# Seven quarter products for eight column pairs of the first up projection, with weight sums added in place by DMAs

## The chip, the cores and the metric

The kernel runs on one core of a Trainium2 chip. Its time is the device time of one execution in microseconds (us). TensorE (PE) multiplies, VectorE (DVE) and ScalarE (ACT) do elementwise work and read PSUM, GpSimd (POOL) does a few additions and can issue DMAs, and SyncE (SP) issues nearly all DMAs. PSUM holds the sums of the matmuls in banks; SBUF holds everything else.

## The reference

A trunk of two decoder layers works on 528 tokens (16 learned ones before 512) of width 1024, all in float32. Each layer is a mixer (one combined projection, four retention heads and four heads of gated linear attention, an output projection) and a gated MLP, each between two RMS norms. The change is in the MLP of the first layer:

```python
def _conv_ffn(h, ffn_up, ffn_conv_w, ffn_conv_b, ffn_down):
    length = h.shape[1]
    u = h @ ffn_up                                   # (528, 1024) @ (1024, 5632)
    up = jnp.pad(u, ((0, 0), (CONV_W - 1, 0), (0, 0)))
    conv = ffn_conv_b + sum(up[:, i:i + length] * ffn_conv_w[i] for i in range(CONV_W))
    a, g = jnp.split(conv, 2, axis=-1)
    return (jax.nn.gelu(a, approximate=True) * g) @ ffn_down
```

The 5632 columns are 22 blocks of 128 for `a` and 22 for `g`. Block i of `a` meets block i of `g` in the product behind the GELU, so the kernel works through 22 column pairs.

## The kernel before

Activations lie with the feature on the partitions and the 528 tokens along the free axis. Precision of float32 is kept by splitting: each activation and each weight is a sum of two float16 numbers, and a product is three matmuls (high x high, high x low, low x high), added up in one PSUM bank (`product_step`, L410). The normalised input of a projection is `xh`, eight tiles (k = 0 to 7) of high and low parts.

A weight block (`Block`, L80) is 1024 rows by 128 columns, 512 KB. SP loads it into a staging buffer (eight of them in layer 0); ACT writes its scaled high part into a *unit* (L110) and DVE its low part (L111). There are ten units. `plan` (L593) lists all blocks in the order of use, and `block` (L622) hands out one of them and, before that, asks for the next ten (`AHEAD`), so loads and conversions run ahead of the matmuls as far as staging buffers and units are free.

`ffn_up` (L1033) goes through the column pairs. `one(key, i, half)` multiplies one block with one part of the tokens (232 in the first half, 296 in the second): 24 matmuls into one of three PSUM banks, which ACT then copies to SBUF as `u` (L1058). `finish(col)` does the convolution of both columns (`conv`: one pass on ACT, L1042, and two on DVE, L1047), the GELU (L1098), and, one pair later, the product and its split into float16 (L1109, L351, L352). The first five pairs (`ULEAD`) run their first token half before the second, because the second half of the norm before them is still on its way; the other pairs run both halves in turn. `tick()` takes one step of whatever generator of background work is waiting.

The order of instructions on each engine is written out by hand only for the opening of the kernel; after it a planner orders them by program order and its own estimates of durations. At run time every engine, and every queue that issues DMAs, takes its instructions strictly in the planned order.

The last down projection (`last_down`) already uses the scheme that the change brings to the up projection: seven products of quarter matrices in place of eight, with sums of weights (there made by DVE, L144) and sums of activations. `w11` to `t4` and `r1`, `r5`, `u2` are its names.

Of the kernel before, what the change touches and what calls it, by code (L numbers as in the profile page):

```python
# [20 lines left out]
DEPTH = 2  # L21
INW = 3600
DFF = 2816
KF = DFF // P
# [7 lines left out]
WN = max(272, L - SPLIT)  # L32
LEVELS = [1, 2, 4, 8, 16, 32, 64]
SX = 8.0
SW = 128.0
SA = 8.0
IXW = 1.0 / (SX * SW)
# [4 lines left out]
UNITS = 10  # L42
# [3 lines left out]
ULEAD = 5  # L46
# [13 lines left out]
HK = KF // 2  # L60
HT = SEQ // 2
PRODUCTS = (("w11", "t1"), ("t2",), ("w22", "t3"), ("w21",), ("t4",))
KPARTS = ((0, 8), (8, 8), (16, 6))


# [5 lines left out]
def cell(pool, shape, dt, tag, name, bufs=None):  # L71

    n = math.prod(shape[1:])
    size = 2 if dt == F16 else 4
    t = pool.tile([shape[0], -(-n * size // CELL) * CELL // size], dt, tag=tag, name=name, **({"bufs": bufs} if bufs else {}))[:, :n]
    names = "abcdef"[: len(shape) - 1]
    return t if len(names) == 1 else t.rearrange(f"p ({' '.join(names)}) -> p {' '.join(names)}", **dict(zip(names, shape[1:])))


class Block:  # L80


    def __init__(self, kern, layer, src, nk, c0, w):
        self.kern, self.src, self.nk, self.c0, self.w = kern, src, nk, c0, w
        self.unit = self.st = None
        self.ahead = 99
        self.layer = layer

    def load(self):
        if self.w < P:  # L90
            st = self.st = self.kern.rank.rearrange("p (k c) -> p k c", c=self.w)
        else:
            st = self.st = cell(self.kern.stage, [P, KD, self.w], F32, *self.kern.stage_of(self.layer))[:, : self.nk]
        load = self.kern.nc.sync.dma_start(st, self.src[:, self.c0 : self.c0 + self.w].rearrange("(k p) c -> p k c", p=P))
        if self.layer:
            self.kern.tc.keep_in_program_order(load)

    def fetch(self):
        if self.unit is not None:
            return  # L100
        nc = self.kern.nc
        if self.st is None:
            self.load()
        st = self.st
        if self.w < P:
            self.unit = cell(self.kern.wpool, [P, self.nk, P // (2 * self.w), 2, self.w], F16, "unit", "unit", UNITS)
            u = self.unit[:, :, 0].rearrange("p k i c -> p i k c")
        else:
            u = self.unit = cell(self.kern.wpool, [P, 2, KD, self.w], F16, "unit", "unit", UNITS)[:, :, : self.nk]
        nc.scalar.activation(u[:, 0], st, AF.Copy, scale=SW)  # L110
        nc.vector.scalar_tensor_tensor(out=u[:, 1], in0=st, scalar=SW, in1=u[:, 0], op0=ALU.mult, op1=ALU.subtract)  # L111
        if self.w < P:
            for j in range(1, self.unit.shape[2]):
                nc.gpsimd.tensor_copy(out=self.unit[:, :, j], in_=self.unit[:, :, 0])


class Quarter:
# [22 lines left out]
    def fetch(self):  # L140
        if self.unit is not None:
            return
        kern, nc, kk = self.kern, self.kern.nc, self.kk
        add = lambda to, x: kern.tc.keep_in_program_order(nc.vector.tensor_tensor(out=to, in0=to, in1=x, op=ALU.add))  # L144
        if self.what == "w11":
            x = self.acc["w11", kk] = self.load(kern.w11_place(kk))
        elif self.what == "w22":
            x = self.acc["w22", kk] = self.load()
        elif self.what == "w21":
            x = self.load()  # L150
        else:
            x = self.acc.pop(("w22", kk)) if self.what == "t3" else self.acc["w11", kk]
            add(x, self.load())
        self.unit = cell(kern.wpool, [P, 2, 2, 512], F16, "unit", "unit", UNITS)[:, :, : self.nk]
        high = nc.scalar.activation(self.unit[:, 0], x, AF.Copy, scale=SW)
        if self.what in ("w11", "t1"):
            kern.tc.keep_in_program_order(high)
        nc.vector.scalar_tensor_tensor(out=self.unit[:, 1], in0=x, scalar=SW, in1=self.unit[:, 0], op0=ALU.mult, op1=ALU.subtract)


class Kern:
# [105 lines left out]
    def mm(self, shape, name="mm"):  # L267
        return self.pmm.tile(shape, F32, tag="mm", name=name)
# [324 lines left out]
    def plan(self):  # L593
        a = self.a
        self.blocks, self.key = [], {}

        def add(key, *args):
            self.key[key] = len(self.blocks)
            self.blocks.append(Block(self, key[0], *args))

        cols = {"rk": C_RK, "rq": C_RQ, "rv": C_RV, "rg": C_RG, "gk": C_GK, "gq": C_GQ, "gv": C_GV, "gr": C_GR}
        for l in range(DEPTH):
            for nm, h in TILES:
                add((l, nm, h), a["w_in"][l], KD, *((C_GA, 16) if nm == "ga" else (cols[nm] + P * h, P)))
            for i in range(KD):
                add((l, "out", i), a["w_out"][l], KD, P * i, P)
            for i in range(KF):
                add((l, "upa", i), a["ffn_up"][l], KD, P * i, P)
                add((l, "upg", i), a["ffn_up"][l], KD, DFF + P * i, P)
            if l < DEPTH - 1:  # L610
                for i in range(KD):
                    for kk, nk in KPARTS:
                        add((l, "dn", i, kk), a["ffn_down"][l][kk * P : (kk + nk) * P], nk, P * i, P)
            else:
                acc = {}
                for group in PRODUCTS:
                    for kk in range(0, HK, 2):
                        for what in group:
                            self.key[l, "dn", what, kk] = len(self.blocks)
                            self.blocks.append(Quarter(self, a["ffn_down"][l], what, kk, min(2, HK - kk), acc))  # L620
# [390 lines left out]
    def out_proj(self, l):  # L1011
# [18 lines left out]
        self.finish(gens[0])  # L1030
        self.xh, self.later = xh, gens[1]

    def ffn_up(self, l):  # L1033
        nc = self.nc
        base = 0 if l < DEPTH - 1 else 14
# [2 lines left out]
        us = {}  # L1038

        def conv(u, c, col):  # L1040
            ci = lambda i: 88 + (l * 3 + i) * 44 + col
            nc.scalar.activation(c[:, lo:L], u[:, lo:], AF.Identity, scale=self.cvec[:, ci(2) : ci(2) + 1],  # L1042
                                 bias=self.cvec[:, l * 44 + col : l * 44 + col + 1])
            for i in (1, 0):
                d = 2 - i
                to = c[:, max(lo, d) :]
                nc.vector.scalar_tensor_tensor(out=to, in0=u[:, max(lo, d) - d : L - d], scalar=self.cvec[:, ci(i) : ci(i) + 1],  # L1047
                                               in1=to, op0=ALU.mult, op1=ALU.add)
# [13 lines left out]
        keep, parts = {}, {nm: [None] * HK for nm in ("x11", "x12", "x22", "s1", "s2", "s3", "s4")}  # L1062
# [52 lines left out]
        for half in range(2):  # L1115
            for i in range(ULEAD):
                one("upa", i, half)
                one("upg", i, half)
                if half:
                    finish(i)  # L1120
            if half == 0:
                self.finish(self.later)
        for i in range(ULEAD, KF):
            for half in range(2):
                one("upa", i, half)
                one("upg", i, half)
            finish(i)
# [3 lines left out]
    def ffn_down(self, l, av):  # L1131
# [176 lines left out]
```

## Time and profile before

| | us |
|---|---|
| median of 3 runs | 1251.44 |
| lowest and highest run | 1250.09, 2556.68 |
| profiled execution, device time | 1250.15 |
| its span in the trace | 1248.4 |
| PE busy | 1227.0 |
| DVE busy | 806.5 |
| ACT busy | 654.2 |
| POOL busy | 157.1 |

The profiled execution lies within 0.1% of the median; the 1.8 us between its time and its span lie outside the trace. Times within the trace count from the start of the span. A row of a group of instructions names its line, engine, operation, the tiles it writes and reads, its shape and count; behind the first bar stand busy time and the mean duration in ns, behind the second the idle time of the engine just before, and what ended it. A row of a stretch gives its length, then the busy time (and count) of PE, the weight loads of PE, DVE, ACT and POOL, then PE's granted clock, the busy share of the DMA engines and the GB/s they moved. A matmul's duration in the trace contains its way through the array; matmuls overlap, so their pace is read from their number in a stretch. The first up projection runs from about 288 to 530 us.

### The profile page before, as it was taken

What the parts mean: (1) busy time and instruction counts of PE and PEld (TensorE: products, weight loads), DVE (VectorE), ACT (ScalarE), POOL (GpSimd) and SP (SyncE); (2) the same over time, 40 slices, a digit from 0 to 9 for tenths busy, and PEclk for the clock granted to TensorE, in tenths of its full rate; (3) what the DMA queues carried; (4) which work ended last, traced back from release to release, by engine and by line L of the source; (5) the groups of instructions that cost most, each with busy time, mean ns of one, the idle gap of its engine ahead of it and who ended that gap; (6) DMA issues with size and microseconds to landing.
All of it is one profiled execution on the core that took longest, in us unless ns stands there. A gap on an engine that the chain in (4) does not pass through costs nothing.

```text
span 1248.4 us, 26366 instructions
## 1 busy us (share of the span) xinstructions
PE 1227.0 (98%) x11106; PEld 1017.4 (81%) x11106; DVE 806.5 (65%) x1414; ACT 654.2 (52%) x1290; POOL 157.1 (13%) x206
## 2 busy tenths in 40 slices
PE   8999999999999999999999999999999999999997
PEld 8788888889888888888878888888798888886443
DVE  5577744467876666613186878434669768887686
ACT  5675445454865555523255744453638556664442
POOL 1012211153000000000032222011520000000001
PEclk9999999999999999999999999999999999999999
DMA  7932221131533333315052332212315333305461
GB/s 203 264 108 86 68 70 52 51 101 36 153 102 94 94 94 93 93 42 139 14 157 73 98 86 67 71 52 69 102 35 153 102 102 102 119 1 181 149 236 68
DMA packets 206827, 124.18 MB, mean 99 GB/s; under 512 B 6688, under 2 KB 194132, under 8 KB 206708
## 3 DMA queue, kind: packets, MB, share of 16 engines
q1 hardware_dynamic: 206548, 121.97, 33.2%
q8 instruction: 87, 1.43, 0.5%
q0 software_dynamic: 160, 0.52, 0.2%
q14 instruction: 32, 0.26, 0.1%
HBM read 120.38 MB, written 2.10 MB: 98 GB/s over the span
## 4 chain that ended last, share of the span: by engine, by line
PE 92%; DVE 3%; POOL 2%; ACT 1%; issue 1%; DVEq 0%; POOLq 0%; ACTq 0%
PE pu L414 12%; PE pu L415 12%; PE pu L413 12%; PE pl L1173 8%; PE pj L413 8%; PE pj L415 7%; PE pj L414 7%; PE pd L413 3%; PE pd L414 3%; PE pd L415 3%; PE po L413 2%; PE po L415 2%; PE po L414 2%; PE lps L841 1%; DVE unit L111 1%
## 5 line engine op out<-in xcount | busy, mean ns | idle before, releaser
L414 PE MATMUL pu<-every,unit 128*128 128x296 f16 (+2 forms) x1408 | 385.7, 275 | 2.1 <-DVE every L352 2.1
L415 PE MATMUL pu<-every,unit 128*128 128x296 f16 (+2 forms) x1408 | 385.7, 275 | 0.0
L413 PE MATMUL pu<-every,unit 128*128 128x296 f16 (+2 forms) x1408 | 384.1, 275 | 0.7 <-ACT every L351 0.7
L111 DVE SCALAR_TENSOR_TENSOR unit<-st,unit 128x1024 f16<-128x1024 f32 x184 | 227.1, 1234 | 162.0 <-ACT unit L110 156.3
L413 PEld LDWEIGHTS <-unit 128*128 128x128 f16 x2912 | 284.7, 98 | 49.2 <-issue 6.9
L415 PEld LDWEIGHTS <-unit 128*128 128x128 f16 x2912 | 284.6, 98 | 46.4 <-issue 3.1
L414 PEld LDWEIGHTS <-unit 128*128 128x128 f16 x2912 | 284.9, 98 | 41.5 <-issue 0.2
L110 ACT ACTIVATE unit<-st 128x1024 f16<-128x1024 f32 x184 | 191.5, 1041 | 127.9 <-PE pu L415 52.6
L415 PE MATMUL pj<-every,unit 128*128 128x296 f16 (+2 forms) x896 | 246.4, 275 | 0.7 <-DVE unit L111 0.7
L413 PE MATMUL pj<-every,unit 128*128 128x296 f16 (+2 forms) x896 | 246.7, 276 | 0.0
L414 PE MATMUL pj<-every,unit 128*128 128x296 f16 (+2 forms) x896 | 246.6, 275 | 0.0
L1058 ACT ACTIVATE u<-pu 128x296 f32<-128x296 f32 (+2 forms) x176 | 66.3, 379 | 95.9 <-PE pu L415 95.8
L415 PE MATMUL pd<-av,unit 128*128 128x232 f16 (+1 forms) x352 | 96.9, 276 | 0.0
L414 PE MATMUL pd<-av,unit 128*128 128x296 f16 (+1 forms) x352 | 96.8, 276 | 0.0
L413 PE MATMUL pd<-av,unit 128*128 128x232 f16 (+1 forms) x352 | 96.8, 276 | 0.0
L379 DVE TENSOR_TENSOR acc<-acc,sq 128x296 f32<-128x296 f32 (+2 forms) x60 | 33.3, 556 | 78.5 <-ACT sq L377 76.5
L347 POOL TENSOR_TENSOR every<-every 128x1 f32<-128x1 f32 (+5 forms) x33 | 38.9, 1181 | 289.2 <-DVE every L346 192.0
L1173 PE MATMUL pl<-unit,fk 128*128 128x512 f16 x330 | 71.4, 379 | 0.0
L1047 DVE SCALAR_TENSOR_TENSOR cg<-u,every,cg 128x527 f32<-128x527 f32 (+1 forms) x88 | 66.5, 756 | 5.5 <-ACT cg L1042 4.3
L415 PE MATMUL po<-merged,unit 128*128 128x296 f16 (+2 forms) x256 | 69.9, 275 | 0.0
L414 PE MATMUL po<-merged,unit 128*128 128x296 f16 (+2 forms) x256 | 69.9, 275 | 0.0
L413 PE MATMUL po<-merged,unit 128*128 128x296 f16 (+2 forms) x256 | 69.7, 275 | 0.0
(225 smaller groups left out, 1502.4 us busy)
## 6 DMA issues: line engine op xcount, KB each, us to landing
st<-in_ffn_up SPq DMA_DIRECT2D x88, 512.0 KB, 3.7
st<-in_w_in SPq DMA_DIRECT2D x56, 512.0 KB, 4.1
st<-in_ffn_down SPq DMA_DIRECT2D x46, 512.0 KB, 3.7
st<-in_w_out SPq DMA_DIRECT2D x16, 512.0 KB, 4.0
st<-in_ffn_down SPq DMA_DIRECT2D x8, 384.0 KB, 3.1
out<-yo SPq DMA_DIRECT2D x8, 256.0 KB, 2.0
xt<-in_x SPq DMA_DIRECT2D x6, 256.0 KB, 6.3
w<-in_ffn_down SPq DMA_DIRECT2D x3, 512.0 KB
```

The costliest lines, as they stand in the source:

```text
L110: nc.scalar.activation(u[:, 0], st, AF.Copy, scale=SW)
L111: nc.vector.scalar_tensor_tensor(out=u[:, 1], in0=st, scalar=SW, in1=u[:, 0], op0=ALU.mult, op1=ALU.subtract)
L347: nc.gpsimd.tensor_tensor(out=r[:w, :n], in0=t[:w, :n], in1=self.mhalf[:w, :n], op=ALU.pow)
L379: eng.tensor_tensor(out=acc[:, :n], in0=acc[:, :n], in1=sq[:, :n], op=ALU.add)
L413: nc.tensor.matmul(ps[:, :n], w[:, 0, kk, :], x[:, 0, n0:n1], start=first, stop=False)
L414: nc.tensor.matmul(ps[:, :n], w[:, 0, kk, :], x[:, 1, n0:n1], start=False, stop=False)
L415: nc.tensor.matmul(ps[:, :n], w[:, 1, kk, :], x[:, 0, n0:n1], start=False, stop=last)
L841: nc.tensor.matmul(dst, x[hs, i, c0 : c0 + w], q, start=(i, j) == (0, 0), stop=i == 1)
L1047: nc.vector.scalar_tensor_tensor(out=to, in0=u[:, max(lo, d) - d : L - d], scalar=self.cvec[:, ci(i) : ci(i) + 1], in1=to, op0=ALU.mult, o ...
L1058: nc.scalar.activation(u[:, n0:n1], ps[:, : n1 - n0], AF.Copy, scale=IXW)
L1173: mm = lambda x, w, **kw: nc.tensor.matmul(ps, x, w, skip_group_check=more, **kw)
```

## The change

In layer 0 the column pairs 7, 9, 11, ... 21 are computed together, `a` block and `g` block as one product of a 1024 x 256 weight with the 528 tokens. All three dimensions are cut in two: rows in 2 x 512 (four k each), columns into the two blocks, tokens in 2 x 264. The four quarter results come out of seven quarter products of 4 k x 3 matmuls each, instead of eight. In the names of the last down projection, with W_ab the quarter of row half a and column block b:

- step 0: w11 = W00 and w22 = W11, loaded by SP into the two halves of a staging buffer
- step 1: t1 = W00 + W01 and t3 = W11 + W01, by two DMAs that POOL issues and that add W01 from DRAM to what lies in the buffer
- step 2: t2 = t1 + W11, by one more adding DMA, and w21 = W10, loaded by SP over t3
- step 3: t4 = t2 + W10, by one more adding DMA

Each step is converted to float16 (ACT, then DVE) into a unit of its own, half a unit for step 3, before the next step changes the buffer. So a pair has four blocks in the plan's list in place of two. `input_sums` makes the four sums of the activations once, on DVE and ACT, as background work during the second token half of the first five pairs. `paired` does the seven products in two banks that are added to after they were read (`pa`: products 1, 3, 5 and 7, `pb`: 2 and 4) and a third (`pd`: product 6); ACT copies the intermediate values r1, r5, u2 and the last result out, DVE forms the other three results from PSUM and those copies. Layer 1 and the other pairs stay as they are.

```diff
+PAIRED = {0: range(7, KF, 2), 1: ()}
+HK2 = KD // 2
+LT = L // 2
...
+class PairPiece:
...
+    def fetch(self):
+        if self.unit is not None:
+            return
+        kern, nc = self.kern, self.kern.nc
+        load = lambda to, *q: nc.sync.dma_start(to, self.quarter(*q))
+        add = lambda to, *q: nc.gpsimd.dma_start(out=to, in_=self.quarter(*q), accum_op=ALU.add)
+        if self.step == 0:
+            self.st = cell(kern.stage, [P, 2, HK2, P], F32, *kern.stage_of(self.layer))
+        st = self.first.st
+        if self.step == 0:
+            load(st[:, 0], 0, 0)
+            load(st[:, 1], 1, 1)
+        elif self.step == 1:
+            add(st[:, 0], 0, 1)
+            add(st[:, 1], 0, 1)
+        elif self.step == 2:
+            add(st[:, 0], 1, 1)
+            load(st[:, 1], 1, 0)
+        else:
+            add(st[:, 0], 1, 0)
+            st = st[:, :1]
+        u = self.unit = cell(kern.wpool, [P, 2, 2, HK2, P], F16, "unit", "unit", UNITS)[:, :, : st.shape[1]]
+        nc.scalar.activation(u[:, 0], st, AF.Copy, scale=SW)
+        nc.vector.scalar_tensor_tensor(out=u[:, 1], in0=st, scalar=SW, in1=u[:, 0], op0=ALU.mult, op1=ALU.subtract)
...
+    def input_sums(self):
...
+        for k in range(0, KD, 2):
+            nc.vector.tensor_tensor(out=xf[:, k : k + 2], in0=xh[:, k : k + 2, 0], in1=xh[:, k : k + 2, 1], op=ALU.add)
+            yield
...
+            nc.vector.tensor_tensor(out=to, in0=x0, in1=x1, op=op)
+            t = parts[:, (2, 0, 1, 3)[i]]
+            nc.scalar.activation(t[:, 0], to, AF.Copy)
+            nc.vector.tensor_tensor(out=t[:, 1], in0=to, in1=t[:, 0], op=ALU.subtract)
+            yield
+
+    def paired(self, units, scale, out):
...
+        def product(ps, step, i, x, more=False):
+            u = units(step)[:, :, i]
+            for k in range(HK2):
+                mm = lambda p, q, **kw: nc.tensor.matmul(ps, u[:, p, k, :], x[k][:, q], skip_group_check=more, **kw)
+                mm(0, 0, start=k == 0 and not more, stop=False)
+                mm(0, 1, start=False, stop=False)
+                mm(1, 0, start=False, stop=k == HK2 - 1)
+            self.tick()
...
+        pa, pb = bank(), bank()
+        product(pa, 0, 0, half(0, 0))
+        r1 = copied(pa)
+        product(pb, 1, 0, self.xsum[1])
+        r5 = copied(pb)
+        product(pa, 2, 0, self.xsum[2], True)
+        u2 = copied(pa)
+        product(pb, 0, 1, self.xsum[4], True)
+        sum_to(1, 0, pb, u2, 1.0, ALU.subtract)
+        product(pa, 1, 1, self.xsum[3], True)
+        sum_to(1, 1, pa, r5, -1.0, ALU.add)
+        pd = bank()
+        product(pd, 2, 1, half(HK2, 0))
+        sum_to(0, 0, pd, r1, 1.0, ALU.add)
+        product(pa, 3, 0, half(HK2, 1), True)
+        nc.scalar.activation(out[0][:, LT:], pa, AF.Copy, scale=scale)
...
         for i in range(ULEAD, KF):
+            if i in PAIRED[l]:
+                for key in ("upa", "upg"):
+                    us[key, i] = cell(self.gen, [P, L], F32, "u", "u", 2 * ULEAD)
+                self.paired(lambda q: self.block(l, "pair", i, q), IXW, (us["upa", i], us["upg", i]))
+                finish(i)
+                continue
```

More of the change, by code (lines that the diff above doesn't have):

```diff
@@ L158, in fetch, with __init__, quarter @@
         nc.vector.scalar_tensor_tensor(out=self.unit[:, 1], in0=x, scalar=SW, in1=self.unit[:, 0], op0=ALU.mult, op1=ALU.subtract)
+class PairPiece:
+    def __init__(self, kern, layer, src, cols, step, first):
+        self.kern, self.layer, self.src, self.cols, self.step = kern, layer, src, cols, step
+        self.first = first or self
+        self.unit = None
+        self.ahead = 99
+    def quarter(self, a, b):
+        return self.src[512 * a : 512 * (a + 1), self.cols[b] : self.cols[b] + P].rearrange("(k p) c -> p k c", p=P)
+    def fetch(self):
[22 more added lines that the diff above has]
+        nc.vector.scalar_tensor_tensor(out=u[:, 1], in0=st, scalar=SW, in1=u[:, 0], op0=ALU.mult, op1=ALU.subtract)
 class Kern:
@@ L607, in plan @@
             for i in range(KF):
+                if i in PAIRED[l]:
+                    first = None
+                    for q in range(4):
+                        self.key[l, "pair", i, q] = len(self.blocks)
+                        self.blocks.append(PairPiece(self, l, a["ffn_up"][l], (P * i, DFF + P * i), q, first))
+                        first = first or self.blocks[-1]
+                    continue
                 add((l, "upa", i), a["ffn_up"][l], KD, P * i, P)
@@ L1031, in out_proj @@
         self.xh, self.later = xh, gens[1]
+    def input_sums(self):
+        nc = self.nc
+        xf = cell(self.keep, [P, KD, L], F32, "xf", "xf", 1)
+        two = cell(self.keep, [P, 2, HK2, LT], F32, "xt", "xt", 1)
+        parts = cell(self.keep, [P, 4, 2, HK2, LT], F16, "xs", "xs", 1)
+        self.xsum = [None] + [[parts[:, i, :, k] for k in range(HK2)] for i in range(4)]
+        xh = self.xroom.bitcast(F16).rearrange("p (k i n) -> p k i n", k=KD, i=2)
+        for k in range(0, KD, 2):
+            nc.vector.tensor_tensor(out=xf[:, k : k + 2], in0=xh[:, k : k + 2, 0], in1=xh[:, k : k + 2, 1], op=ALU.add)
+            yield
+        x = lambda a, b: xf[:, HK2 * b : HK2 * (b + 1), LT * a : LT * (a + 1)]
+        for i, (to, x0, x1, op) in enumerate(((two[:, 1], x(0, 0), x(1, 0), ALU.subtract), (two[:, 0], x(1, 0), x(1, 1), ALU.subtract),
+                                              (x(0, 0), two[:, 0], x(0, 0), ALU.subtract), (x(0, 1), x(0, 0), x(0, 1), ALU.add))):
+            nc.vector.tensor_tensor(out=to, in0=x0, in1=x1, op=op)
[3 more added lines that the diff above has]
+            yield
@@ new lines, in paired, with copied, sum_to @@
+    def paired(self, units, scale, out):
+        nc = self.nc
+        half = lambda k0, a: [self.xh[k][:, :, LT * a : LT * (a + 1)] for k in range(k0, k0 + HK2)]
+        bank = lambda: self.mm([P, WN], "pp")[:, :LT]
+        def product(ps, step, i, x, more=False):
[6 more added lines that the diff above has]
+            self.tick()
+        def copied(ps):
+            t = self.g([P, LT], F32, "part")
+            nc.scalar.activation(t, ps, AF.Copy, scale=scale)
+            return t
+        def sum_to(o, a, ps, y, sign, op):
+            nc.vector.scalar_tensor_tensor(out=out[o][:, LT * a : LT * (a + 1)], in0=ps, scalar=sign * scale, in1=y, op0=ALU.mult, op1=op)
+        pa, pb = bank(), bank()
[14 more added lines that the diff above has]
+        nc.scalar.activation(out[0][:, LT:], pa, AF.Copy, scale=scale)
@@ L1122, in ffn_up @@
                 self.finish(self.later)
+                if PAIRED[l]:
+                    self.spawn(self.input_sums())
         for i in range(ULEAD, KF):
+            if i in PAIRED[l]:
+                for key in ("upa", "upg"):
+                    us[key, i] = cell(self.gen, [P, L], F32, "u", "u", 2 * ULEAD)
+                self.paired(lambda q: self.block(l, "pair", i, q), IXW, (us["upa", i], us["upg", i]))
+                finish(i)
+                continue
             for half in range(2):
```

## The prediction

> **What bounds the kernel now.** I read the page's busy times first, then its chain of waits, then two-column stretches of the stage that changes.
>
> ```profile
> span 1248.4 us, 26366 instructions
> PE 1227.0 (98%) x11106; PEld 1017.4 (81%) x11106; DVE 806.5 (65%) x1414; ACT 654.2 (52%) x1290; POOL 157.1 (13%) x206
> PE 92%; DVE 3%; POOL 2%; ACT 1%; issue 1%; DVEq 0%; POOLq 0%; ACTq 0%
> ```
> TensorE is busy for 98% of the span and is 92% of the chain that ended last: work taken off PE counts in full as long as nobody makes PE wait. The first up projection, cut into stretches of 21.5 us, which is two column pairs:
>
> ```profile
> core 0: us, PE busy (x) PEld busy (x) DVE busy (x) ACT busy (x) POOL busy (x), PEclk, DMA share, GB/s
> 400.00:421.50 21.50, 21.50 (x193) 18.69 (x192) 13.58 (x16) 11.89 (x20) 0.00 (x0) 1.00 0.34 99
> 421.50:443.00 21.50, 21.50 (x193) 18.66 (x191) 13.58 (x16) 11.89 (x20) 0.00 (x0) 1.00 0.33 99
> ```
> PE never idles, at clock 1.00; DVE has 13.58 us of work in 21.5 (63%), ACT 11.89 (55%), POOL nothing, and the DMA engines are a third busy. So the stage is bound by PE alone, with room on every other engine.
>
> **The change, part by part.** *Matmuls removed.* A column pair is now 2 columns x 2 token parts x 8 k x 3 = 96 matmuls, 48 of 232 tokens and 48 of 296, 264 on average. In the paired form it is 7 products x 4 k x 3 = 84 matmuls of 264. The rows give 21.5/193 = 0.1114 us for one of that mean length; 12 fewer save 1.34 us a pair, 10.7 us over the eight pairs (columns 7, 9, ... 21). A product then lasts 12 x 0.1114 = 1.34 us, a paired column 9.4, and two columns 20.2 instead of 21.5. I use the mean because issue is the pace and the weight loads stay under it (18.69 of 21.5).
>
> *Vector and scalar work added.* The stage's own shapes (361 to 500 us) and, below, an add of the last down projection, a sum out of PSUM and the square sums:
>
> ```profile
> L111 DVE SCALAR_TENSOR_TENSOR unit<-st,unit 128x1024 f16<-128x1024 f32 x26 | 31.9, 1226 | 40.0 <-ACT unit L110 40.0
> L110 ACT ACTIVATE unit<-st 128x1024 f16<-128x1024 f32 x25 | 26.3, 1052 | 25.5 <-PE pu L415 25.5
> L1058 ACT ACTIVATE u<-pu 128x296 f32<-128x296 f32 x26 | 10.6, 408 | 10.6 <-PE pu L415 10.6
> L1058 ACT ACTIVATE u<-pu 128x232 f32<-128x232 f32 x26 | 9.2, 356 | 24.7 <-PE pu L415 24.7
> ```
> ```profile
> L144 DVE TENSOR_TENSOR w<-w,st 128x1024 f32<-128x1024 f32 x9 | 11.0, 1219 | 0.0
> L1191 DVE SCALAR_TENSOR_TENSOR yo<-pl,part 128x512 f32<-128x512 f32 x6 | 4.0, 685 | 0.0
> L379 DVE TENSOR_TENSOR acc<-acc,sq 128x232 f32<-128x232 f32 x22 | 11.1, 505 | 58.4 <-ACT sq L377 57.6
> ```
> The weights of a pair become 3.5 units instead of 2: DVE 1.5 x 1.226 = +1.84, ACT 1.5 x 1.052 = +1.58. The four evacuations by ACT (2 x 0.408 + 2 x 0.356 = 1.53) become four copies of 264, again 1.53. DVE gets three sums of 264 out of PSUM, between 0.505 (232, from SBUF) and 0.685 (512, from PSUM); I take 0.5 each, +1.5. Per two columns DVE goes to 13.58 + 3.3 = 16.9 of 20.2 (84%), ACT to 13.5 (67%). Neither becomes the bound: cost nothing, hidden beside PE. Were the cover gone, 3.3 us a pair would be 27 us.
>
> *The input sums* are 12 DVE passes over 1056 elements (about 12 x 1.25 = 15 us, by L144) and 4 on ACT (4.3 us), once, spread over the second half of the first five columns:
>
> ```profile
> 320.00:330.00 10.00, 10.00 (x82) 7.75 (x80) 9.70 (x13) 9.86 (x15) 0.00 (x0) 1.00 0.67 190
> 330.00:340.00 10.00, 10.00 (x84) 7.94 (x82) 10.00 (x14) 8.47 (x14) 0.00 (x0) 1.00 0.69 200
> 340.00:350.00 10.00, 10.00 (x91) 8.59 (x89) 9.66 (x15) 7.08 (x12) 0.00 (x0) 1.00 0.37 108
> 360.00:500.00 140.00, 140.00 (x1247) 121.60 (x1245) 87.66 (x105) 76.64 (x131) 0.00 (x0) 1.00 0.32 95
> ```
> They fall where DVE is already full (29.4 of 30 us) and yet PE does not idle, because weights are converted up to ten blocks ahead. The 15 us drain later: 360 to 500 alone has 52 us of idle DVE, and the pairs take 27 of the stage's. Column 7 starts near 361 (first evacuation of column 5, below, less its product, plus two columns). Bounds: 0, and the 11 us or so that DVE cannot fit before 361; I take 1, since PE idled nowhere in that crowd.
>
> ```profile
> 341.87 0.35 ACT L1058 ACTIVATE u<-pu 128x232 f32<-128x232 f32 x1
> ```
> *Hand-offs inside a pair: the new wait.* Two banks are refilled on top of what ACT or DVE still has to read: product 3 waits for r1, 4 for r5, 5 for u2 (ACT), 7 for the sum out of product 5 (DVE). Each has one product, 1.34 us, as cover. Today's hand-off:
>
> ```profile
> 484.21 0.26 PE L415 MATMUL pu<-every,unit 128*128 128x232 f16 x1
> 484.51 0.36 ACT L1058 ACTIVATE u<-pu 128x232 f32<-128x232 f32 x1 [1.90 <-PE pu L415]
> ```
> ```profile
> ACT u L1058 <- PE pu L415: 35.3, 26, 1.9
> SPq L94 <- DVE unit L111: 128.8, 26, 7.0
> ```
> From the start of a product's last matmul to ACT's start is 0.30 us, the copy 0.38: 0.68, which leaves 0.66 of cover before the way back to PE; I count 0.6. Of the 52 evacuations between 360 and 500 only 26 found ACT waiting; the rest stood behind something, at worst a conversion (1.05). A busier ACT hits that oftener. Bounds per hand-off: 0, and 1.2 us (a conversion and one more op ahead, less the cover). I take 0.5 a pair, since one hand-off in three loses some 0.4; 4 us in all. Behind PE's wait stand the next products only; the third bank holds product 6, which can be placed into such a gap.
>
> *The adds.* Per pair three loads of 256 KB on SP (w11, w22, later w21), and four adding DMAs of 256 KB on POOL: two, one, one, each step waiting for the conversion (ACT, then DVE: 2.3 us) of the step before. No adding DMA is in this trace. Nearest rows:
>
> ```profile
> st<-in_ffn_up SPq DMA_DIRECT2D x88, 512.0 KB, 3.7
> out<-yo SPq DMA_DIRECT2D x8, 256.0 KB, 2.0
> every<-in_post_ffn_norm POOLq DMA_DIRECT2D x2, 256.0 KB, 7.3
> ```
> ```profile
> L1161 POOL DMA_DIRECT2D every<-in_post_ffn_norm x2 | 1.3, 650 | 213.9 <-PE pu L415 213.9
> ```
> ```profile
> 1134.00:1140.00 6.00, 6.00 (x39) 3.61 (x38) 2.90 (x4) 2.86 (x5) 1.30 (x2) 1.00 0.70 235
> ```
> So 2.0 to 7.3 us from issue to landing, and 0.65 of POOL an issue; I take 7.3, the only row with POOL as issuer and this size. A pair's first conversion can begin when the unit ten blocks back is free: that of step 2 two pairs before, 32.2 us ahead (2 x 20.2 less 6 products). Chain: 2.3 conversion, 8.0 for two adds, 2.3, 7.9, 2.3, 7.9, 1.3 = 32.0 us, so step 3 is ready 0.2 us before the pair starts, and its product comes 6 products (8.1 us) later. Step 2 has 12 us to spare, step 1 more. Cost taken: 0, hidden by that slack; gone at about 10 us a step. On POOL nothing is queued behind the adds before the next norm, after this stage. On SP the w21 load waits for step 1's conversion, and the loads behind it wait too: SP already waits 128.8 us of 140 for a freed staging buffer there, and a pair's buffer, held some 30 us, is one of eight.
>
> Here the Trainium skill speaks (DMA: Bandwidth & Descriptors, "Anatomy of one DMA"): a DMA that POOL issues takes about 2.0 us plus its bytes at 436 GB/s. An estimate by that page is 2.6 us for 256 KB; the trace has 7.3, on DMA engines that were 70% busy just then. With 2.6 the slack would grow by 14 us and the sum would stay.
>
> *The sum:* 1250.15 (the profiled execution; median 1251.44, so 1.3 lower) - 10.7 + 4 + 1 = 1244.5; I say 1245 for the median. A 0.5% gain cannot be told from no change by the 2% (25 us) that a measurement of this kernel resolves.
>
> **The rivals.** *Slower: ACT stuck behind an add.* ACT takes its instructions in the order the planner wrote. If the planner counts on an early landing (2.0) and the add needs 7.3 or more, the next conversion stands at ACT's head, and the evacuations behind it; PE runs out of banks after one product. There are 24 add steps. For: the trace times no adding DMA, and its one row with POOL as issuer is the slowest of its size. Against: ACT is 67% busy, so conversions drift back. If 5.3 us are late and 3.3 are caught by drift and banks, 2 us each are 48 us: 1293. It makes the kernel slower by 2% from 31/24 = 1.3 us of PE a step. Chance 0.16.
>
> *POOL locked out by DVE.* An add's issue could be held while DVE works, and DVE is at work 84% of the time here. The only POOL issues in the trace, 0.65 us each, ran beside a DVE that was busy for 2.90 of the 6 us in the row above, so they exclude nothing. Behind one 1.226 us operation each, an add step grows by some 2.5 us at most: three are 7.5, inside the 8 us of slack. Only with ACT stuck as above is it paid: 24 x 1.3 = 31 us, about 1276. Chance 0.04. The Trainium skill has this (SBUF — State Buffer, "SBUF: two separate sides"): DVE's two-port modes block POOL from writing descriptors; no row here shows it.
>
> *Hand-offs eat the gain.* If half the bound is paid, 4 x 0.6 = 2.4 us a pair, 19 us: 1250.15 - 10.7 + 19 + 1 = 1259. For: products are half as long as today's groups (24 matmuls, 2.7 us). Against: 0.6 us of cover and a spare bank. Chance 0.18.
>
> *DVE late for column 7:* 11 us once: 1254. Chance 0.05.
>
> **Numbers.** Forecast 0.57, its own range 1240 (hand-offs free) to 1252. Faster by over 2% would need 25 us where 10.7 are all that PE gives up: 0.01. Slower by over 2%: both ACT cases, 0.20. Within: 0.79. The range leaves out the worst of the ACT case (0.12) and what is below 1239 (0.05): 1239 to 1280.
>
> **What would show it.** PE's matmuls fewer by 96; two columns of the stage in about 20.5 us; DVE near 84% there; PE idle of some 0.5 us a pair, released by ACT or DVE. ACT's conversions waiting for a DMA, with PE idle for microseconds behind them, would prove the first rival. Adds landing after more than 10 us would break the slack, and with it the forecast.

## The result and the profile after

| | before | after |
|---|---|---|
| median, us | 1251.52 | 1301.2 |
| ratio to before, 95% interval | | 1.0403 [1.0382, 1.0423] |
| span of the profiled execution, us | 1248.4 | 1299.1 |
| PE busy / span less PE busy, us | 1227.0 / 21.4 | 1237.6 / 61.5 |

The kernel became 4% slower. One of the four runs before took 2556.68 us; the ratio is formed without it. The page of the changed kernel, the lines that answer to those shown of before, with the slices of granted clock, one group of matmuls and the adding DMAs:

```profile
span 1299.1 us, 26404 instructions
...
PE 1237.6 (95%) x11010; PEld 1017.9 (78%) x11010; DVE 839.9 (65%) x1466; ACT 668.4 (51%) x1310; POOL 197.9 (15%) x238
...
PEclk9999999999979888899999999999999999999999
...
PE 54%; DVE 2%; issue 1%; ACT 1%; POOL 0%; DMA 0%; DVEq 0%; POOLq 0%; ACTq 0%
...
L1115 PE MATMUL pp<-xs,unit 128*128 128x264 f16 x384 | 64.9, 340 | 39.9 <-ACT part L1123 39.9
...
st<-in_ffn_up POOLq DMA_DIRECT2D x32, 256.0 KB, 5.0
```
The 96 matmuls are gone (11106 to 11010). Yet PE is busy for 10.6 us more, and idle for 40.1 us more. One group holds nearly all of that idle time: matmuls of the new stage that waited for ACT's copies of intermediate results (L1123, `copied`). The granted clock falls in just the slices of this stage. Three stretches of two columns each, a paired one and a plain one:

```profile
390.00:417.60 27.60, 24.44 (x216) 20.87 (x214) 17.00 (x23) 14.61 (x25) 5.27 (x5) 1.00 0.55 102
417.60:445.20 27.60, 20.88 (x154) 16.54 (x153) 14.78 (x21) 12.03 (x21) 4.93 (x4) 0.81 0.50 95
445.20:472.80 27.60, 22.95 (x181) 18.56 (x179) 15.92 (x22) 13.17 (x23) 5.12 (x4) 0.88 0.54 103
```
Two columns take about 27.6 us instead of 21.5 before, and PE, which filled its stretches before, idles in all three. So this is a stage of waits. Who waits for whom between 300 and 590 us (total, times, longest):

```profile
ACT unit L201 <- DMA st<-in_ffn_up: 92.8, 24, 5.6
...
PE pp L1115 <- ACT part L1123: 39.9, 15, 9.2
```
The high conversions of the new units (L201) held ACT 24 times, once for each of the 24 add steps, for 92.8 us. How long one step of the chain is, and how little ACT has been given to do in it, stands in ACT's timeline (start, duration, engine, line, operation; in brackets the idle time before and its releaser):

```profile
402.16 0.37 ACT L1123 ACTIVATE part<-pp 128x264 f32<-128x264 f32 x1
404.67 1.06 ACT L201 ACTIVATE unit<-st 128x1024 f16<-128x1024 f32 x1 [2.13 <-DMA st<-in_ffn_up]
405.63 0.37 ACT L1123 ACTIVATE part<-pp 128x264 f32<-128x264 f32 x1
405.90 0.63 ACT L395 ACTIVATE av<-cg 128x528 f16<-128x528 f32 x1
406.43 0.38 ACT L1123 ACTIVATE part<-pp 128x264 f32<-128x264 f32 x1
412.00 0.63 ACT L201 ACTIVATE unit<-st 128x512 f16<-128x512 f32 x1 [5.18 <-DMA st<-in_ffn_up]
```
Step 3's conversion follows step 2's by 7.33 us: the conversions, an add's issue and its landing lie between. The planner had put three operations of 1.4 us in all into that time. So ACT stood for 5.18 us. These two conversions belong to the pair whose first product starts at 420.90, so with DVE's low part (412.66 to 413.35) its units were ready 7.5 us early. What they held up is the pair before. The pair at 420.90 was held up in its turn by the conversions of the next one, first in PE's timeline, then in ACT's:

```profile
420.90 1.51 PE L1115 MATMUL pp<-every,unit 128*128 128x264 f16 x12
422.25 1.51 PE L1115 MATMUL pp<-xs,unit 128*128 128x264 f16 x12
423.60 1.51 PE L1115 MATMUL pp<-every,unit 128*128 128x264 f16 x12
430.88 2.80 PE L1115 MATMUL pp<-xs,unit 128*128 128x264 f16 x12 [5.77 <-ACT part L1123]
```
```profile
425.46 1.06 ACT L201 ACTIVATE unit<-st 128x1024 f16<-128x1024 f32 x1 [5.58 <-DMA st<-in_ffn_up]
...
430.46 0.37 ACT L1123 ACTIVATE part<-pp 128x264 f32<-128x264 f32 x1
433.24 1.06 ACT L201 ACTIVATE unit<-st 128x1024 f16<-128x1024 f32 x1 [2.42 <-DMA st<-in_ffn_up]
```
Product 1 ends at 422.4, and its copy r1 could have begun there. It ran at 430.46: a conversion that waited 5.58 us for a DMA stood ahead of it, and behind that conversion nearly four us of other ACT work had piled up, which came first as well. PE did two products in free banks (the one at 423.60 is product 6, drawn forward) and then stood for 5.77 us. After that pause it was also slow: 12 matmuls took 2.80 us where the three products before took 1.51. The same place in stretches:

```profile
427.00:430.00 3.00, 0.00 (x0) 0.00 (x0) 2.96 (x5) 2.40 (x6) 1.27 (x1) 0.90 0.28 79
430.00:432.00 2.00, 1.12 (x6) 0.76 (x6) 1.85 (x3) 0.83 (x2) 0.00 (x0) 0.50 1.02 136
436.00:438.00 2.00, 2.00 (x11) 1.39 (x10) 0.64 (x3) 0.00 (x0) 1.29 (x1) 0.50 0.00 0
440.00:442.00 2.00, 2.00 (x23) 1.97 (x21) 0.81 (x2) 1.08 (x2) 0.00 (x0) 1.00 0.06 7
```
The granted clock (the column behind POOL's) is 0.50 from 430 to 438, with 11 matmuls in 2 us, and 1.00 at 440, with 23.

With a version of the same matmuls that hardly stalls (both edits with 10, 8, 4, 2, below: PE 1216.8 us busy) the 50.7 us of span come apart: 1216.8 - 1227.0 = -10.2 from fewer matmuls, 1237.6 - 1216.8 = +20.8 from longer matmuls, 61.5 - 21.4 = +40.1 of idle PE. Most of the 20.8 is the clock: in the trace six stretches of the stage have a clock of 0.50, PE works 36.7 us in them, and half of that, 18.4 us, is an estimate of what the clock cost.

### The profile page after: what moved, and what is told of

Read it like the earlier page. It is cut to its first block, busy times and chain, and to the rows that moved or that the text cites. A ratio compares the mean times of both kernels' runs of the same rounds, so it can differ in the third digit from the quotient of the medians.

```text
span 1299.1 us, 26404 instructions
## 1 busy us (share of the span) xinstructions
PE 1237.6 (95%) x11010; PEld 1017.9 (78%) x11010; DVE 839.9 (65%) x1466; ACT 668.4 (51%) x1310; POOL 197.9 (15%) x238
## 4 chain that ended last, share of the span: by engine, by line
PE 54%; DVE 2%; issue 1%; ACT 1%; POOL 0%; DMA 0%; DVEq 0%; POOLq 0%; ACTq 0%
PE pl L1294 8%; PE pu L458 6%; PE pu L459 6%; PE pu L457 6%; PE pj L457 4%; PE pj L458 4%; PE pj L459 4%; PE pd L459 3%; PE pd L458 3%; PE pd L457 3%; PE po L457 1%; PE po L458 1%; PE po L459 1%; DVE unit L114 1%; PE pp L1115 1%
## 5 line engine op out<-in xcount | busy, mean ns | idle before, releaser
L458 PE MATMUL pu<-every,unit 128*128 128x296 f16 (+2 forms) x1152 | 314.8, 274 | 2.1 <-DVE every L396 2.1
L459 PE MATMUL pu<-every,unit 128*128 128x296 f16 (+2 forms) x1152 | 314.8, 274 | 0.0
L457 PE MATMUL pu<-every,unit 128*128 128x296 f16 (+2 forms) x1152 | 313.1, 274 | 0.7 <-ACT every L395 0.7
L114 DVE SCALAR_TENSOR_TENSOR unit<-st,unit 128x1024 f16<-128x1024 f32 (+1 forms) x168 | 206.2, 1234 | 113.3 <-ACT unit L113 107.2
L113 ACT ACTIVATE unit<-st 128x1024 f16<-128x1024 f32 (+1 forms) x168 | 173.7, 1039 | 89.5 <-PE pd L459 34.8
L1115 PE MATMUL pp<-xs,unit 128*128 128x264 f16 x384 | 64.9, 340 | 39.9 <-ACT part L1123 39.9
L1171 ACT ACTIVATE u<-pu 128x296 f32<-128x296 f32 (+2 forms) x144 | 53.5, 376 | 53.8 <-PE pu L459 53.5
L201 ACT ACTIVATE unit<-st 128x1024 f16<-128x1024 f32 (+1 forms) x32 | 30.3, 946 | 92.8 <-DMA st<-in_ffn_up 92.8
L202 DVE SCALAR_TENSOR_TENSOR unit<-st,unit 128x1024 f16<-128x1024 f32 (+1 forms) x32 | 34.9, 1090 | 64.7 <-ACT unit L201 64.7
L184 POOL DMA_DIRECT2D st<-in_ffn_up x32 | 41.1, 1416 | 203.6 <-DVE unit L202 168.1
```

The lines of the kernel that those rows point to most:

```text
L184: add = lambda to, *q: nc.gpsimd.dma_start(out=to, in_=self.quarter(*q), accum_op=ALU.add)
L457: nc.tensor.matmul(ps[:, :n], w[:, 0, kk, :], x[:, 0, n0:n1], start=first, stop=False)
L458: nc.tensor.matmul(ps[:, :n], w[:, 0, kk, :], x[:, 1, n0:n1], start=False, stop=False)
L459: nc.tensor.matmul(ps[:, :n], w[:, 1, kk, :], x[:, 0, n0:n1], start=False, stop=last)
L1115: mm = lambda p, q, **kw: nc.tensor.matmul(ps, u[:, p, k, :], x[k][:, q], skip_group_check=more, **kw)
L1171: nc.scalar.activation(u[:, n0:n1], ps[:, : n1 - n0], AF.Copy, scale=IXW)
```

## The experiments

The theory after the result: ACT takes its instructions in the planner's order, and conversions of the next pair that wait for an add stand ahead of the copies that the current pair needs. The rivals: the adding DMAs do harm by themselves (traffic, POOL, DVE), the seven products cost more in hand-offs than they save, or the units come too late for their products. Edits are shown against the changed kernel.

**No chain, no adds.** Each step loads quarters into a staging buffer of its own. The sums of the weights are left out; products, conversions, copies and sums out of PSUM stay.

```diff
...
-            self.st = cell(kern.stage, [P, 2, HK2, P], F32, *kern.stage_of(self.layer))
-        st = self.first.st
...
+        st = cell(kern.stage, [P, 2, HK2, P], F32, *kern.stage_of(self.layer))
+        for i, q in enumerate((((0, 0), (1, 1)), ((0, 1), (0, 1)), ((1, 1), (1, 0)), ((1, 0),))[self.step]):
+            load(st[:, i], *q)
...
```


> The four steps of a pair each load their quarters into a staging buffer of their own, with plain loads on SP and no adds (the sums of weights are left out, so the products are of single quarters). Matmuls, conversions, copies and sums stay as in the changed kernel, and so do the bytes loaded. Theory A (ACT's planned order holds a conversion that waits for an add ahead of the copies that PE needs): the waits of ACT for a DMA go, PE's clock stays at 1.00, 1241 to 1249 us (10.7 us of matmuls saved, some 4 us of hand-offs). Theory B (the short products and their hand-offs, or the added work on DVE and ACT, cost the time): 1259 us or more, with PE still waiting for L1123.

Measured: 1243.83 us, 0.9944 [0.9929, 0.9958]. Its waits, the stretch that the prediction worked from, and the last matmul of layer 0's down projection, that of the kernel before first (this kernel's copies are L1113, its paired matmuls L1105):

```profile
PE pp L1105 <- ACT part L1113: 2.6, 8, 1.2
```
```profile
360.00:500.00 140.00, 137.81 (x1222) 119.26 (x1221) 108.33 (x147) 89.72 (x152) 0.00 (x0) 1.00 0.49 142
```
```profile
642.96 0.29 PE L415 MATMUL pd<-av,unit 128*128 128x296 f16 x1
```
```profile
635.85 0.29 PE L449 MATMUL pd<-av,unit 128*128 128x296 f16 x1
```
No wait of ACT for a DMA is left, and PE waits 2.6 us for copies, 8 times. PE ends layer 0 7.1 us earlier than before; with the 2.6 us of waits that makes 9.7 of the 10.7 predicted. What was predicted of the seven products holds here to about 1 us. The loss comes with the chain of adds alone, and the hand-off rival has fallen.

**The chain with plain loads.** The adds become loads on SP into the same place, so each step still waits for the conversion of the step before. The additions are left out.

```diff
-        add = lambda to, *q: nc.gpsimd.dma_start(out=to, in_=self.quarter(*q), accum_op=ALU.add)
+        add = lambda to, *q: nc.sync.dma_start(to, self.quarter(*q))
```


> As the changed kernel, in place and in the same four steps with the same waits, but the four adding DMAs are plain loads on SP that write over the buffer (the additions are left out). Theory A: a step is shorter by POOL's issue (1.27 us) and whatever adding costs in landing, so ACT's wait of 3.9 us a step falls to 1 to 3 us and the time lies between, 1250 to 1280 us. If the adding alone were at fault (theory C: an add is slow in itself), the loss would go altogether: below 1250. If the chain of four steps in one buffer is at fault whatever its DMAs: 1290 or more.

Measured: 1268.28 us, 1.0139 [1.0122, 1.0156]. Its waits:

```profile
ACT unit L201 <- DMA st<-in_ffn_up: 43.8, 24, 4.7
...
PE pp L1115 <- ACT part L1123: 23.2, 15, 3.6
```
With plain loads from SP the same 24 waits remain at half the length, and PE stands 23.2 us instead of 39.9, never over 3.6 at a time. So a chain of loads in one buffer costs 24.5 us over the version without a chain, with no adding DMA at all. The rest would then be the longer step that the adding DMAs make (5.0 us from issue to landing, 3.5 for these loads); the next two runs test the other possibility, that the adds do harm by themselves.

**The adds without the chain, twice.** Both take the first experiment's kernel (sums of weights left out) and issue the same 32 adds where nobody reads the result: first into one spare buffer, with nothing to wait for,

```diff
...
+        ghost = kern.ghost()
+        for i, q in enumerate(((), ((0, 1), (0, 1)), ((1, 1),), ((1, 0),))[self.step]):
+            add(ghost[:, i], *q)
...
```
(`ghost`, not shown, makes one buffer of zeros.)

> As the kernel with four plain steps (no sums of weights), plus the same 32 adding DMAs on POOL, which now add into a buffer of their own that nobody reads. Theory A: nobody waits for them, so within 3 us of that kernel. Theory C (the adds cost by themselves: the DMA engines' traffic, POOL's issue beside DVE): at least 15 us above it.

then into each step's own buffer, right behind its second conversion:

```diff
...
+        for i, q in enumerate((((0, 1), (0, 1)), ((1, 1),), ((1, 0),), ())[self.step]):
+            add(st[:, i], *q)
```


> The four plain steps again (no sums of weights, 1243.83 us without adds), with the 32 adding DMAs issued on POOL right behind each step's conversion, into that step's own buffer, which nobody reads any more. In the run before this one the adds had nothing to wait for and all ran ahead of the stage, so it did not test this. Theory A (only the wait at ACT's head costs): within 4 us of 1243.83. Theory C (the adds cost by themselves, through the DMA engines, POOL's issue or DVE): 1258 us or more.

Measured: 1308.43 us, 1.0458 [1.0442, 1.0474], and 1243.51, 0.9944 [0.9927, 0.996]. By its time alone the first would speak for the rival (at least 15 us above), but it says nothing of the stage: with nothing to wait for, the planner put all adds at the start of the kernel, one after the other in one buffer. Its POOL's timeline, the last of them and what follows:

```profile
145.45 1.29 POOL L184 DMA_DIRECT2D ghost<-in_ffn_up  x1 [4.17 <-DMA ghost<-in_ffn_up]
146.24 1.39 POOL L943 TENSOR_TENSOR room<-room,a 128x264 f32<-128x264 f32 x1
```
The mixer's POOL work had to stand behind them until 146 us, and the first copy of the first up projection came at 354.0 us instead of 290.2 in the kernel before, which is nearly all of the 64.6 us lost: the same fault as in the change, on another engine. The second version has the adds in their stage. Its stretch and its DMA row:

```profile
360.00:500.00 140.00, 137.81 (x1222) 119.31 (x1220) 108.29 (x147) 89.74 (x151) 32.00 (x25) 1.00 0.92 189
```
```profile
st<-in_ffn_up POOLq DMA_DIRECT2D x32, 256.0 KB, 5.9
```
PE and DVE do to 0.1 us what they did without the adds, though the DMA engines are 92% busy and an add lands in 5.9 us. Traffic, POOL's issuing and DVE are excluded as causes by themselves: what is left is who waits for the adds.

**The full change, with other places for the conversions.** `ahead` says how many blocks before its use a step's work is written into the program (99 stands for the common limit of ten). The kept order is a note to the planner that the high conversion stays where the program has it. Four kernels, all with the sums of the weights made in full: both edits with two spacings, and each edit alone.

```diff
-        self.ahead = 99
+        self.ahead = (10, 8, 4, 2)[step]
...
-        nc.scalar.activation(u[:, 0], st, AF.Copy, scale=SW)
+        kern.tc.keep_in_program_order(nc.scalar.activation(u[:, 0], st, AF.Copy, scale=SW))
```
Kept order and 10, 8, 6, 4 (`10 - 2 * step`):

> The changed kernel in full, with two edits in the order alone: step q of a pair is asked for 10 - 2q blocks ahead (not 10 for all), and ACT's part of each conversion may not be placed ahead of what was written before it on ACT. Conversions of one pair then stand 8 to 12 us apart in ACT's order, against the 7.4 us that a step takes. Theory A: most of ACT's waits for DMAs go (from 93 us to under 25), 1244 to 1262 us, perhaps below the kernel before. Theory D (the chain itself is too long, units come late whatever the order): 1290 or more, PE waiting for units.

Kept order and 10, 8, 4, 2, as in the diff:

> The changed kernel in full, with ACT's part of the conversions kept behind what was written before it, and step q asked for 10, 8, 4 and 2 blocks ahead, which by the pace of the matmuls is 12, 12 and 11 us apart (8 to 12 in the run with 10 - 2q, which left 41 us of waits, 5 us each at the third step). Theory A: those waits go too, ACT waits under 15 us for DMAs, 1244 to 1254 us. If a time of 1265 or more comes out with few waits on ACT, something else than the order costs (late units, or hand-offs).

Kept order alone, `ahead` at 99:

> The changed kernel with one of the two edits of the run that came out at 1244.6 us: ACT's part of a pair's conversions is kept behind what was written before it on ACT, but all four steps are still asked for ten blocks ahead. Where a conversion may earliest stand is then set by the pace of the units (1 to 3 us apart at steps 0 to 2), not by the 7.4 to 9 us of a step. Theory A with the spacing as the cause: little is gained, 1285 to 1302 us, ACT waiting over 60 us for DMAs. If keeping the order is what matters: below 1260.

The spacing 10, 8, 4, 2 alone:

> The other edit alone: steps asked for 10, 8, 4 and 2 blocks ahead, the planner free to place ACT's parts earlier. It has the two last full conversions of a pair one convolution apart in places. Theory A: waits return where it moved a conversion forward, 1250 to 1285 us, in proportion to ACT's waits for DMAs. If asking late is enough: 1243 to 1248, with ACT's waits under 15 us.

| | median, us | ratio, 95% interval | ACT L201 for DMA: us, times, longest | PE for ACT copies: us, times, longest |
|---|---|---|---|---|
| change | 1301.2 | 1.0403 [1.0382, 1.0423] | 92.8, 24, 5.6 | 39.9, 15, 9.2 |
| kept order alone | 1301.67 | 1.0406 [1.0389, 1.0423] | 89.0, 24, 6.4 | 46.1, 16, 8.5 |
| kept order, 10, 8, 6, 4 | 1271.49 | 1.0165 [1.0149, 1.018] | 41.2, 11, 7.3 | 10.2, 2, 5.3 |
| spacing alone | 1259.08 | 1.0063 [1.0048, 1.0079] | 36.9, 9, 5.5 | 14.0, 7, 5.3 |
| kept order, 10, 8, 4, 2 | 1244.6 | 0.9951 [0.9937, 0.9966] | 3.8, 1, 3.8 | 3.5, 1, 3.5 |

The last one's span and busy times, its stage and its waits:

```profile
span 1242.8 us, 26394 instructions
...
PE 1216.8 (98%) x11010; PEld 1008.6 (81%) x11010; DVE 837.1 (67%) x1466; ACT 668.6 (54%) x1310; POOL 196.2 (16%) x238
...
st<-in_ffn_up POOLq DMA_DIRECT2D x32, 256.0 KB, 5.9
```
```profile
360.00:500.00 140.00, 136.51 (x1204) 118.43 (x1202) 112.10 (x151) 92.36 (x152) 33.24 (x26) 0.99 0.76 142
```
```profile
ACT unit L201 <- DMA st<-in_ffn_up: 3.8, 1, 3.8
...
PE pp L1115 <- ACT part L1123: 3.5, 1, 3.5
```
The same adds, landing no sooner (5.9 us against 5.0), cost next to nothing once each conversion stands in ACT's order behind the work that fills its add's time. 23 of 24 waits are gone, and 56.6 us with them. This version beats both kernels, the one before by 0.5%, and its interval excludes 1. The order is the cause, then. It takes both edits: keeping ACT in program order while all steps are asked for ten blocks ahead changes nothing, and with the spacing alone nine conversions still stood waiting.

With 10, 8, 6, 4 it was eleven, PE waited for DVE's sums too (11.4 us, 5 times), and the time missed its expectation of 1244 to 1262. In two places of its trace ACT stood 5.35 us (until 425.74) and 5.07 us (until 448.70) at the third step of a pair, whose add landed 8.7 and 8.5 us after its issue, against a median of 5.9. SP issued several loads within two us of these adds; that they made the adds late was not tested.

**Other engines for the chain.** First the sums on POOL: all four quarters loaded by SP into two staging buffers, five POOL additions of 512 elements a pair, the order by the planner.

```diff
...
+        pool = lambda to, x0, x1, op=ALU.add: nc.gpsimd.tensor_tensor(out=to, in0=x0, in1=x1, op=op)
+        if self.step == 1:
+            for i in range(2):
+                pool(st[:, i], st[:, i], other[:, 0])
...
+            pool(other[:, 0], st[:, 1], other[:, 0], ALU.subtract)
+            pool(other[:, 0], other[:, 0], st[:, 0])
+        elif self.step == 3:
+            pool(other[:, 1], other[:, 1], other[:, 0])
...
```


> The changed kernel with the sums of weights made by five additions of 512 elements a pair on POOL, from four quarters that SP loads ahead into two staging buffers; no DMA is waited for inside a pair's chain. Order as the planner makes it, nothing pinned. Theory A: additions on an engine are short (about 1.6 us of POOL each, by its 0.9 us for 296 elements), so ACT hardly stands: 1242 to 1252 us. If a chain in steps is at fault whatever makes the sums: 1270 or more.

Measured: 1269.34 us, 1.0146 [1.0131, 1.0161]. Its waits, and the passes of the convolution on DVE (shortest, median and longest ns), which in the changed kernel were never over 768:

```profile
ACT av L395 <- DVE cg L1222: 26.5, 16, 3.5
...
PE pp L1115 <- ACT part L1123: 21.0, 11, 6.6
...
ACT unit L201 <- POOL st L190: 9.7, 9, 2.2
```
```profile
L1160 DVE SCALAR_TENSOR_TENSOR ca<-u,every,ca x36: 752/766/1775, 358.3 to 547.9; 128x527 f32<-128x527 f32 x18, 128x526 f32<-128x526 f32 x18
```
The time missed the expected 1242 to 1252 and lies beside what was expected if any chain is at fault (1270 or more), so this run does not speak for the theory by its time. ACT's wait at the conversions did fall from 92.8 to 9.7 us, as the theory has it for a short step. But ACT now stood for DVE, 26.5 us, and again PE for the copies behind. Some DVE passes take twice their time beside a POOL addition (last section). How much of the 26.5 us is due to that and how much to the new order was not taken apart.

Then the adds as in the change, but the high conversion on POOL, so that ACT waits for no DMA:

```diff
-        nc.scalar.activation(u[:, 0], st, AF.Copy, scale=SW)
+        nc.gpsimd.tensor_scalar(out=u[:, 0], in0=st, scalar1=SW, scalar2=None, op0=ALU.mult)
```


> The changed kernel with the high part of a pair's conversions made by POOL in place of ACT; adds, chain and DVE's low part as they were. Theory A: ACT never stands behind an add, PE's copies come in time, and what is left is DVE standing behind POOL (three of the seven hand-offs are DVE's): 1248 to 1275 us. If ACT's order had nothing to do with it: 1295 to 1310, as the changed kernel.

Measured: 1320.92 us, 1.0561 [1.0545, 1.0577], above both expectations. Its waits and POOL's group:

```profile
POOL unit L201 <- DMA st<-in_ffn_up: 81.2, 20, 5.1
...
ACT av L395 <- DVE cg L1222: 32.3, 15, 5.3
PE pp L1115 <- POOL unit L201: 31.4, 10, 5.2
...
PE pp L1115 <- ACT part L1123: 11.3, 7, 5.1
```
```profile
L201 POOL TENSOR_SCALAR unit<-st 128x1024 f16<-128x1024 f32 (+1 forms) x32 | 82.0, 2566 | 116.6 <-DMA st<-in_ffn_up 84.5 <-PE pu L459 21.5 <-ACT cg L1155 3.6
```
PE's wait for ACT's copies shrinks from 39.9 to 11.3 us: the wait for the DMA went to POOL. But a conversion takes 2.57 us there instead of 1.06, a step with one add 9.2 us instead of 7.3 (385.94 to 395.18 in its trace), and now PE waits for the units themselves (31.4 us). Here the slack of the data, which the change had, is used up. How much of that is the longer step, and how much POOL's own order, in which issues of adds now stand behind conversions, was not taken apart.

## Why the prediction was wrong

**The step that failed** is "Cost taken: 0, hidden by that slack; gone at about 10 us a step". The slack was real. A step with one add took 7.3 us; the whole chain of the pair at 420.90 ran from 386.84 to 413.35, 26.5 us where 32.0 had been said; and PE did not wait for a unit in the views above. But slack of the data only says when the products have their weights. The conversions wait on ACT, whose order is fixed, and what stands behind them there are the copies on which PE's next product depends. The right question for that term was how much ACT work the order has between two conversions (1.4 us in the place shown) against the length of a step (7.3).

**The rival that decided** was on record as "ACT stuck behind an add", with a chance of 0.16. It was put down on the argument that conversions "drift back" since ACT is only 67% busy. They cannot: they drift in time, not in order, and all 24 waits stayed. Its condition was not quite what happened: it asked for a landing of 7.3 us or more, and 5.0 were enough, since the order had so little between two conversions. What landing the planner had counted on is in no trace. Its price of 48 us of idle PE (24 steps of 2 us) came near the 40.1 measured partly by luck: PE waited 15 times, from 0.9 to 9.2 us. Its time of 1293 was too low, because a term was missing from every case: after many of these pauses PE worked at half clock, which is most of another 20.8 us. The range ended at 1280, as the worst of this rival had been cut off from it.

**The other terms held.** They are measured by the runs without the chain.
- Matmuls -10.7: -10.2 in PE's busy time (1216.8 against 1227.0; -9.1 and -10.5 in the run without adds and the one with adds that nobody reads), and 7.1 + 2.6 = 9.7 by the end of layer 0, so 0.2 to 1.6 us less than said. Products of 264 tokens start 1.35 us apart (420.90, 422.25, 423.60), said 1.34.
- Hand-offs +4: 2.6, eight times, at most 1.2 each, which is the bound given for one. The version with both edits and 10, 8, 4, 2 has a single one, of 3.5 us, and so above that bound: the copy stood behind two conversions (365.99 and 366.93 us) that waited for no DMA. The rival that they eat the gain (1259) is refuted.
- Input sums +1: nothing. PE has no gap where they run, nor before column 7, so the rival with DVE late falls as well:

```profile
320.00:360.00 40.00, 40.00 (x340) 33.10 (x339) 31.57 (x38) 25.87 (x39) 5.33 (x4) 1.00 0.47 99
```
- DVE 84%, ACT 67% of the stage: 108.33 and 89.72 of 140 us, 77% and 64%: both lower than said, and neither became the bound.
- An add's landing, taken as 7.3 us from the nearest row: 5.0. POOL's issue, taken as 0.65: 1.27. Times to landing count from the start of the issue, so the chain's 7.9 counted the issue twice; two adds, put at 8.0, would be 8.6 by the same two figures. The estimate by the Trainium skill (DMA: Bandwidth & Descriptors, "Anatomy of one DMA") had been 2.6 us; the measurement lies between it and the row. The 7.3 was on the safe side for the slack and warned of nothing. Nor would a shorter landing have saved the forecast: the plain loads landed in 3.5 us, and ACT still waited 43.8 us.
- POOL locked out by DVE: an issue takes 1.27 us beside a DVE busy for 2.96 of 3 us (427 to 430 above), as it does beside a DVE with little to do (436 to 438, 1.29 and 0.64). Not seen.

The sum of 1244.5 is close to what the change gives when ACT's order is right (1244.6). That the two agree to 0.1 us is partly luck: 4 us in small hand-offs and 1 us for the input sums had been said, and there it is one pause of 3.5 us, with matmuls that saved 0.5 us less than said.

## What to carry to other kernels

When an instruction gets a wait on a long chain, look at what stands behind it on its own engine, in the planned order, and not only at when its result is needed: results that were ready 7.5 us early in the place shown cost 50 us here. Compare the length of one step of the chain with the work that the order has between its two ends, and place the steps so that they agree; here that was worth more than the shorter landing of plain loads (1244.6 against 1268.28 us). The pauses of TensorE, 39.9 us in 15, cost about half as much again in matmuls that ran longer, most of it at a lower clock.

## What the runs showed of the hardware

**The clock after a pause.** The pause of 5.77 us was followed by a granted clock of 0.50 for some nine us of work (430 to 439), with a further short pause in it. The length of a pause alone does not tell whether the clock falls. The changed kernel, twice, then the chain with plain loads:

```profile
406.05 2.86 PE L1115 MATMUL pp<-xs,unit 128*128 128x264 f16 x24 [1.96 <-ACT part L1123]
...
513.73 1.87 PE L1115 MATMUL pp<-xs,unit 128*128 128x264 f16 x12 [2.35 <-ACT part L1123]
517.05 5.05 PE L1115 MATMUL pp<-xs,unit 128*128 128x264 f16 x24 [1.46 <-ACT part L1123]
```
```profile
414.65 2.86 PE L1115 MATMUL pp<-xs,unit 128*128 128x264 f16 x24 [3.57 <-ACT part L1123]
```
After 1.96 us, and in the other run after 3.57 us, 24 matmuls take 2.86 us, the full pace. After pauses of 2.35 and 1.46 us they take 5.05: the clock is 0.50 from 514.8 to 521.5. The Trainium skill (TensorE: Matmul & The Clock Gate, "What's actually happening") has the clock halved after an idle window of about 3.4 us and back after about as much busy time. The rows differ from that: a pause of 2.35 us was enough for the fall, one of 3.57 us was not, and the way back took longer than 3.4 us here. What decides it was not tested.

**DVE beside POOL additions.** In the run with POOL's sums a convolution pass of 0.77 us took up to 1.775. One place, both engines:

```profile
416.72 1.67 POOL L190 TENSOR_TENSOR st<-st 128x512 f32<-128x512 f32 x1 [5.31 <-DVE unit L202]
417.18 2.58 DVE L1160 SCALAR_TENSOR_TENSOR ca<-u,every,ca 128x527 f32<-128x527 f32 x2
```
Two passes beside the addition take 2.58 us, where two took 1.56 in the changed kernel. POOL's issuing of adds did nothing of the kind (no pass over 768 ns in the changed kernel). The Trainium skill (SBUF — State Buffer, "SBUF: two separate sides") describes the first as a port pair that one of the two engines holds for a whole instruction; the rows agree with it.
